# Weight sums moved one product ahead, z loaded into eight buffers, products of zeros before the first unit, and several steps of the first head moved

## The chip, the cores and the metric

The kernel runs on one core of a Trainium2 chip. The metric is the device time of one execution in microseconds; for the kernel before it is the median of three runs. A profile is one further execution with the hardware profiler on, and its span runs from the first to the last instruction that it recorded.

## The reference

One encoder layer on 528 rows of 2048 columns (16 meta tokens and 512 positions), cut here to what matters:

```
proj = h @ w_in                                  # u, g_ssm, q, k, v, g_sb, 1024 columns each
z    = gelu(s5_scan(u))                          # 64 groups of a diagonal state space model
hg   = z @ w_glu + b_glu
y_ssm = (hg[:, :1024] * sigmoid(hg[:, 1024:]) * silu(g_ssm)) @ w_branch_ssm
y_sb  = (stick_breaking_attention(q, k, v) * silu(g_sb)) @ w_branch_sb
gates = sigmoid(h @ w_gate + b_gate)             # 2048 x 4096 weights
mixed = gates[:, :2048] * y_ssm + gates[:, 2048:] * y_sb
out   = layer_norm(ALPHA * h + mixed @ w_out)
```

## The kernel before

Every operand of a large product is split into a high part (a cast to a narrower float32 form, on ScalarE) and a low part (the difference, on VectorE), and `mm3` issues three matmuls for each pair of operands: high by high, low by high, high by low. So each chunk of weights (128 by 1024, 512 KB, one DMA on SyncE's queue) needs a `copy` on ScalarE (line 171, tile `whi`) and a `split_lo` on VectorE (line 96, tile `wlo`) before TensorE can use it.

The work is a sequence of slots written by `slot()`. A slot uses one chunk in 8 pieces of 3 or more matmuls. At its start, `prep_upto` emits the copy and the split of the chunk that is used two slots later; the finish of the previous slot (`pend`) is emitted after that, or ahead of it where `soon=True`. At the fifth piece `load_upto` emits the DMA of the chunk five slots ahead. `schedule()` puts other work (VectorE tables, loads, the state space model, attention) at a piece number counted from the call. Each engine takes its instructions in the order in which they were emitted, and waits on data alone, so emission order is the whole schedule.

The stages in order: the first head's unit pair (u and v together, 16 pieces), its gate, k and q; then seven more heads, each with the state space and attention stages of the head before woven in; then eight units of g_ssm, in which the input is reloaded and its block sums are made for the next stage (`load_b`, `sums_b`); then the gates; then z times w_glu; the two branch products; and the output product with the layer norm.

The gates are 16 pairs (`pair(j)`), each seven products of 1024 by 128 weights on 256 columns (a seven-product scheme for a two by two block product). The order of the products is x = 0 to 6; x = 1, 2 and 3 use the block sums T2, T1 and T3, the others the input itself. The weight factors are: chunk 11 for x = 0; s2 = 21 + 22 - 11 for x = 1; s1 = 21 + 22 for x = 2; 11 - 21 for x = 3; 12 for x = 4; 12 - s2 for x = 5; 22 for x = 6. `factor()` (lines 142 to 161) emits the VectorE sums just ahead of the copy that needs them. The finishes e0 to e6 move results out of three accumulators: e0 is a ScalarE copy, e1, e3, e5 and e6 have VectorE additions, e3 to e6 a sigmoid on ScalarE, and e5 and e6 start a store from ScalarE's queue. Products x = 3, 5 and 6 accumulate onto an accumulator that an earlier finish has to read first.

During the last pair's x = 4, `open_z` frees the block sums and `load_z` (line 1177) is scheduled eight times, three pieces apart: a DMA of one 128 by 512 tile of z into a single buffer (`zt`, bufs=1), a copy on ScalarE (line 1180, `zh`) and a split on VectorE (`zl`). The stage that follows multiplies piece k by tile k of z.

In the first head, `params_v` (sines, cosines and an exponential, up to 52 scheduled steps on VectorE), `params_g` (on GpSimd) and `params_w` (a table of powers and its followers, up to 37 scheduled steps on VectorE) are put at pieces 10 to 26, 26 and 27 to 54 of the first head's 64 pieces. The splits of the input's 16 tiles (`split_x`, tiles `Xh`, `Xl`) are at pieces 0 to 13, tile c being needed at piece c. The first head's state space products s3 (line 750) and s5 (line 779) stand at pieces 44 and 50 of the second head; s5 needs the PSUM buffer that s3b empties with an addition (tile `X<-aux,dd`), and six 128 by 576 operations of `f3` on VectorE stand at piece 46, ahead of s3b.

Of the kernel before, what the change touches and what calls it, by code (L numbers as in the profile page):

```python
# [16 lines left out]
P = 128  # L17
# [11 lines left out]
NT = 8  # L29
# [9 lines left out]
def kernel(  # L39
# [55 lines left out]
    def tt(out, a, b, op, eng=V):  # L95
        eng.tensor_tensor(out, a, b, op)  # L96
# [29 lines left out]
    def load_upto(f):  # L126
        while issued[0] <= min(f, NFAC - 1):
            i = issued[0]
            pr = pair_of(i)
            if pr is None:  # L130
                raws[i] = load_raw(chunk_of(i))
            else:
                c = GATES + 4 * pr[0]
                w = sev.setdefault(pr[0], {})
                if pr[1] == 0:
                    w["11"], w["21"] = load_raw(c), load_raw(c + 2)
                    w["22"] = load_raw(c + 3, sev["p"], "r22", bufs=2)
                elif pr[1] == 1:
                    w["12"] = load_raw(c + 1)
            issued[0] += 1  # L140

    def factor(w, x):
        if x == 0:
            return w["11"]
        if x == 1:
            w["s1"] = sev["p"].tile([P, 1024], F32, tag="s1", name="s1")
            w["s2"] = sev["p"].tile([P, 1024], F32, tag="s2", name="s2")
            tt(w["s1"], w["21"], w["22"], ALU.add)
            tt(w["s2"], w["s1"], w["11"], ALU.subtract)
            return w["s2"]  # L150
        if x == 2:
            return w["s1"]
        if x == 3:
            tt(w["21"], w["11"], w["21"], ALU.subtract)
            return w["21"]
        if x == 4:
            return w["12"]
        if x == 5:
            tt(w["s2"], w["12"], w["s2"], ALU.subtract)
            return w["s2"]  # L160
        return w["22"]

    def prep_upto(f):
        while prepped[0] <= min(f, NFAC - 1):
            i = prepped[0]
            pr = pair_of(i)
            t = raws.pop(i) if pr is None else factor(sev[pr[0]], pr[1])
            hp, lp = held.get(i, (hi_p, lo_p))
            h = hp.tile([P, 1024], F32R, tag="hi", name="whi")
            lo = lp.tile([P, 1024], F32R, tag="lo", name="wlo")  # L170
            A.copy(h, t)  # L171
            split_lo(lo, t, h)
            his[i], los[i] = h, lo
            prepped[0] += 1
# [55 lines left out]
    with tc.manual_schedule():  # L230
# [48 lines left out]

        load_x(0, 1)  # L280
# [340 lines left out]
        def store_pv():  # L621
# [8 lines left out]
            + steps(gv_, 10, 26, 52)  # L630
            + [(26, lambda: drain(params_g()))]
            + steps(gw_, 27, 54, 37)
            + [(55, store_pv)]
# [64 lines left out]
        def ssm_stages(i):  # L698
# [147 lines left out]
            if i == 0:  # L846
                a = [(24, s1), (27, s1b), (29, s2(0)), (31, s2(1)), (33, s2(2)), (44, s3), (46, s3b), (52, s4)]
            return [(0, s0)] + a + [
                (50, s5), (52, s5a), (55, s5b), (57, s5c), (66, s7), (69, s7b), (71, s8), (74, s9)]
# [202 lines left out]
        for i in range(NT):  # L1052
# [52 lines left out]
            if i < NT - 1:  # L1105
                f1, f2, f3 = ssm_load(i + 1)
                schedule([(54, f1), (61, f3), (72, f2)])
# [69 lines left out]
        def load_z(j):  # L1177
            t = zst["p"].tile([P, S], F32, tag="zt", bufs=1, name="zt")
            SP.dma_start(out=t, in_=zd[j])
            A.copy(zst["h"][:, j, :], t)  # L1180
            split_lo(zst["l"][:, j, :], t, zst["h"][:, j, :])

        def pair(j):
# [46 lines left out]
            for x, (o, bh, bl, first_) in enumerate(ops):  # L1230
# [6 lines left out]
                if j == KT - 1 and x == 4:  # L1237
                    schedule([(0, open_z)] + [(1 + 3 * k, lambda k=k: load_z(k)) for k in range(NT)])
# [30 lines left out]
        def fin_ga(a, j):  # L1269
            hold["a"] = a  # L1270
            hold["t2"] = tmpl("zt")
# [261 lines left out]
```

## Time and profile before

| what | value |
|---|---|
| device time, median of 3 runs (lowest, highest) | 1505.92 us (1505.59, 1507.81) |
| the profiled execution's own time | 1507.89 us |
| its span, first to last instruction | 1506.1 us |
| granted TensorE clock, mean over the span | 0.988 |
| TensorE matmul busy | 1440.1 us (96%) |
| VectorE busy | 942.0 us (63%) |
| ScalarE busy | 482.0 us (32%) |
| GpSimd busy | 48.8 us (3%) |
| DMA | 196.50 MB, mean 130 GB/s |

Busy time counts a matmul from its start to the modelled end of its pipeline, so neighbouring matmuls overlap and a busy TensorE may still be spacing its matmuls too widely. The distance between the starts of neighbouring matmuls says more: it shows the clock and each wait. The clock is given as a share of 2.4 GHz, so 1.00 is the higher of its two levels and 0.50 the lower, 1.2 GHz.

### The profile page before, as it was taken

To read this page: it belongs to the slowest core of one execution; us is meant where nothing else is said; L and a number is where in the kernel's file an instruction comes from. 1 tells how busy PE (TensorE), PEld (TensorE's weight loads), DVE (VectorE), ACT (ScalarE), POOL (GpSimd) and SP (SyncE) were. 2 spreads that over 40 slices of the span, in tenths; PEclk is the share of its full clock that TensorE was granted. 3 is DMA by queue.
4 is the path that set the end of the run, shared out by engine and by line. 5 is a ranking of instruction groups with operands and counts; after the bars stand their busy time and mean duration, and the time that the engine had idled before them with its cause. 6 is when DMAs were issued, how large, how long until landed. Compare 5 with 4: busy or idle time off the path is not lost.

```text
span 1506.1 us, 22031 instructions
## 1 busy us (share of the span) xinstructions
PE 1440.1 (96%) x9040; PEld 1295.2 (86%) x9040; DVE 942.0 (63%) x1397; ACT 482.0 (32%) x764; POOL 48.8 (3%) x95
## 2 busy tenths in 40 slices
PE   7999999999999999998999999996999999999996
PEld 7989999999999898887999999995788888888885
DVE  8887767666767677577666666664454444423357
ACT  5322323233232323234444444433332222221120
POOL 0830000000000000000000000000000000000000
PEclk9999999999999999999999999998899999999998
DMA  7345253434434343462333233233454444474323
GB/s 250 117 129 142 85 141 96 135 105 118 126 114 107 113 116 118 122 219 92 121 131 125 100 133 133 95 124 120 160 150 151 141 151 134 136 208 153 98 98 112
DMA packets 96357, 196.50 MB, mean 130 GB/s; under 512 B 28416, under 2 KB 41984, under 8 KB 95488
## 3 DMA queue, kind: packets, MB, share of 16 engines
q1 hardware_dynamic: 77552, 177.20, 38.5%
q10 hardware_dynamic: 18704, 17.90, 3.5%
q8 instruction: 71, 1.16, 0.3%
q14 instruction: 30, 0.25, 0.1%
HBM read 172.78 MB, written 22.28 MB: 130 GB/s over the span
## 4 chain that ended last, share of the span: by engine, by line
PE 67%; DVE 17%; ACT 8%; issue 5%; DMA 2%; ACTq 0%; SPq 0%; DVEq 0%
PE acc L177 18%; PE acc L178 18%; PE acc L179 18%; ACT whi L171 6%; DVE wlo L96 5%; DVE s L96 4%; PE aux L177 3%; PE aux L179 2%; PE aux L178 2%; DVE u L96 2%; DVE raw L96 1%; DMA zt<-zd 1%; PE aux L818 1%; PE aux L779 1%; PE aux L814 1%
## 5 line engine op out<-in xcount | busy, mean ns | idle before, releaser
L177 PE MATMUL acc<-Xh,whi 128*128 128x256 f32 (+2 forms) x1664 | 520.9, 313 | 6.7 <-ACT whi L277 4.6
L96 DVE TENSOR_TENSOR wlo<-raw,whi 128x1024 fp32r<-128x1024 f32 (+1 forms) x242 | 294.9, 1220 | 362.6 <-ACT whi L171 355.4
L178 PE MATMUL acc<-Xl,whi 128*128 128x256 f32 (+2 forms) x1664 | 515.0, 309 | 2.3 <-DVE Xl L96 2.2
L179 PE MATMUL acc<-Xh,wlo 128*128 128x256 f32 (+2 forms) x1664 | 514.0, 309 | 0.0
L171 ACT CAST whi<-raw 128x1024 fp32r<-128x1024 f32 x238 | 247.7, 1049 | 463.6 <-PE acc L178 311.0
L177 PEld LDWEIGHTS acc<-Xh,whi 128*128 128x128 f32 x1664 | 316.3, 190 | 22.3 <-ACT whi L277 4.6
L178 PEld LDWEIGHTS acc<-Xl,whi 128*128 128x128 f32 x1664 | 316.0, 190 | 17.2 <-DVE Xl L96 3.5
L179 PEld LDWEIGHTS acc<-Xh,wlo 128*128 128x128 f32 x1664 | 315.6, 190 | 15.5
L96 DVE TENSOR_TENSOR wlo<-s,whi 128x1024 fp32r<-128x1024 f32 x48 | 58.8, 1225 | 69.8 <-ACT whi L171 69.8
L171 ACT CAST whi<-s 128x1024 fp32r<-128x1024 f32 x48 | 50.3, 1048 | 89.0 <-DVE s L96 81.5
L177 PE MATMUL acc<-zh,whi 128*128 128x512 f32 x128 | 53.2, 416 | 13.4 <-ACT zh L1180 7.8
L177 PE MATMUL acc<-T3h,whi 128*128 128x256 f32 x128 | 37.4, 292 | 17.4 <-DVE u L96 17.4
L178 PE MATMUL acc<-zl,whi 128*128 128x512 f32 x128 | 52.9, 413 | 0.3 <-DVE zl L96 0.2
L179 PE MATMUL acc<-zh,wlo 128*128 128x512 f32 x128 | 52.2, 408 | 0.0
L179 PE MATMUL acc<-oh,wlo 128*128 128x512 f32 x128 | 49.8, 389 | 0.0
L178 PE MATMUL aux<-wlo,mh 128*128 128x512 f32 x128 | 49.8, 389 | 0.0
L177 PE MATMUL aux<-whi,mh 128*128 128x512 f32 x128 | 49.8, 389 | 0.0
L179 PE MATMUL aux<-whi,ml 128*128 128x512 f32 x128 | 49.8, 389 | 0.0
L178 PE MATMUL acc<-wlo,mh 128*128 128x512 f32 x128 | 49.8, 389 | 0.0
L178 PE MATMUL acc<-sl,whi 128*128 128x512 f32 x128 | 49.8, 389 | 0.0
L178 PE MATMUL acc<-ol,whi 128*128 128x512 f32 x128 | 49.8, 389 | 0.0
L179 PE MATMUL acc<-sh,wlo 128*128 128x512 f32 x128 | 49.8, 389 | 0.0
(274 smaller groups left out, 2310.1 us busy)
## 6 DMA issues: line engine op xcount, KB each, us to landing
raw<-wst SPq DMA_DIRECT2D x238, 512.0 KB
gt<-gtd SPq DMA_DIRECT2D x32, 256.0 KB
xb<-xT SPq DMA_DIRECT2D x16, 264.0 KB
X<-brep SPq DMA_DIRECT2D x8, 512.0 KB
X<-pvd SPq DMA_DIRECT2D x16, 256.0 KB
X<-sd SPq DMA_DIRECT2D x8, 512.0 KB
gtd<-ga ACTq DMA_DIRECT2D x16, 256.0 KB
gtd<-gb ACTq DMA_DIRECT2D x16, 256.0 KB
```

The lines of the kernel that those rows point to most:

```text
L96: eng.tensor_tensor(out, a, b, op)
L171: A.copy(h, t)
L177: PE.matmul(o, ah, bh, start=start, stop=False, **kw)
L178: PE.matmul(o, ah, bl, start=False, stop=False, **kw)
L179: PE.matmul(o, al, bh, start=False, stop=stop, **kw)
L779: PE.matmul(vp[:, g, 0:NK], W["vt"][:, g].rearrange("p r q -> p (r q)"), ut[:, g * NK:g * NK + NK], start=True, stop=True,)
L814: PE.matmul(yp[:, g, 0:SK], W["ot"][:, g].rearrange("p t c -> p (t c)"), hs[:, g * NK + MK - 1:g * NK + MK - 1 + SK], start=True, stop=False,)
L818: PE.matmul(yp[:, g, 0:SK], W["mt"][:, g, :], ut[:, g * NK + MK:g * NK + MK + SK], start=False, stop=True,)
```

## The change

It does these things:

- The sums of the seven-product factors are emitted one product earlier than the copy that needs them: behind the ScalarE copy of the product before and ahead of its split. The loads follow: chunks 11 and 22 of a pair are now issued two slots earlier and chunk 21 one slot earlier, chunk 12 in the same slot as before; 22 goes ahead of 21.
- `zt` has eight buffers. All eight loads of z are issued at the start of the last pair's x = 4; the copies and splits come at pieces 10, 12 and so on to 22, and 23. The later user of the tag `zt` in `fin_ga` uses the eight buffers too.
- Ahead of the first loads a tile of zeros is set on VectorE and TensorE multiplies it 14 times, 256 columns each, into a PSUM tile that nothing reads.
- `params_v` goes to pieces 14 to 29, `params_g` to 29, `params_w` to 30 to 55, the store of its result from 55 to 56.
- For the first head s3, s3b and s4 move from pieces 44, 46, 52 to 47, 49, 55, and every state space step from s5 on moves by 3 pieces. For every head the loads and tables of the next head (f1, f3, f2) move from pieces 54, 61, 72 to 57, 62, 74.

```diff
@@ load_upto
-                if pr[1] == 0:
-                    w["11"], w["21"] = load_raw(c), load_raw(c + 2)
-                    w["22"] = load_raw(c + 3, sev["p"], "r22", bufs=2)
-                elif pr[1] == 1:
+                n_, x = pr
+                c = GATES + 4 * n_
+                w = sev.setdefault(n_, {})
+                nx = sev.setdefault(n_ + 1, {})
+                if i == GATES:
+                    load_first(w, c)
+                    load_second(w, c)
+                if x == 1:
                     w["12"] = load_raw(c + 1)
+                elif x == 5 and n_ < NSEV - 1:
+                    load_first(nx, c + 4)
+                elif x == 6 and n_ < NSEV - 1:
+                    load_second(nx, c + 4)
...
-    def factor(w, x):
...
+    def load_first(w, c):
+        w["11"] = load_raw(c)
+        w["22"] = load_raw(c + 3, sev["p"], "r22", bufs=2)
+
+    def load_second(w, c):
+        w["21"] = load_raw(c + 2)
+
+    summed = [GATES]
+
+    def sums_upto(f):
+        while summed[0] <= min(f, GATES + 7 * NSEV - 1):
+            n_, x = pair_of(summed[0])
+            w = sev[n_]
+            if x == 0:
+                w["s1"] = sev["p"].tile([P, 1024], F32, tag="s1", name="s1")
+                tt(w["s1"], w["21"], w["22"], ALU.add)
+            elif x == 1:
+                w["s2"] = sev["p"].tile([P, 1024], F32, tag="s2", name="s2")
+                tt(w["s2"], w["s1"], w["11"], ALU.subtract)
+            elif x == 2:
+                tt(w["21"], w["11"], w["21"], ALU.subtract)
+            elif x == 4:
+                tt(w["s2"], w["12"], w["s2"], ALU.subtract)
+            summed[0] += 1
+
+    FACTOR = ("11", "s2", "s1", "21", "12", "s2", "22")
@@ prep_upto
-            t = raws.pop(i) if pr is None else factor(sev[pr[0]], pr[1])
+            t = raws.pop(i) if pr is None else sev[pr[0]][FACTOR[pr[1]]]
...
             A.copy(h, t)
+            if GATES - 1 <= i + 1:
+                sums_upto(i + 1)
             split_lo(lo, t, h)
@@ ahead of load_x(0, 1)
+        wz = tp.tile([P, 256], F32R, name="wz")
+        V.memset(wz.bitcast(F32), 0.0)
+        wo_ = aux()
+        for _ in range(14):
+            PE.matmul(wo_[:, 0:256], wz[:, 0:P], wz, start=True, stop=True)
@@ first head's schedule
-            + steps(gv_, 10, 26, 52)
-            + [(26, lambda: drain(params_g()))]
-            + steps(gw_, 27, 54, 37)
-            + [(55, store_pv)]
+            + steps(gv_, 14, 29, 52)
+            + [(29, lambda: drain(params_g()))]
+            + steps(gw_, 30, 55, 37)
+            + [(56, store_pv)]
@@ ssm_stages
-                a = [..., (44, s3), (46, s3b), (52, s4)]
+                a = [..., (47, s3), (49, s3b), (55, s4)]
+            y = 3 if i == 0 else 0
             return [(0, s0)] + a + [
-                (50, s5), (52, s5a), (55, s5b), ...]
+                (50 + y, s5), (52 + y, s5a), (55 + y, s5b), ...]
@@ next head's loads
-                schedule([(54, f1), (61, f3), (72, f2)])
+                schedule([(57, f1), (62, f3), (74, f2)])
@@ load_z
-            t = zst["p"].tile([P, S], F32, tag="zt", bufs=1, name="zt")
+            t = zst["p"].tile([P, S], F32, tag="zt", bufs=NT, name="zt")
             SP.dma_start(out=t, in_=zd[j])
+            zst["t", j] = t
+
+        def split_z(j):
+            t = zst.pop(("t", j))
             A.copy(zst["h"][:, j, :], t)
             split_lo(zst["l"][:, j, :], t, zst["h"][:, j, :])
@@ pair(KT - 1), x == 4
-                    schedule([(0, open_z)] + [(1 + 3 * k, lambda k=k: load_z(k)) for k in range(NT)])
+                    schedule([(0, open_z)] + [(0, lambda k=k: load_z(k)) for k in range(NT)]
+                             + [(10 + 2 * k, lambda k=k: split_z(k)) for k in range(NT - 1)] + [(23, lambda: split_z(NT - 1))])
```

## Rows read from the trace of the kernel before

**Rows 1.** Busy time by stretch: start and end of the stretch, its length, then busy time and count for TensorE's matmuls, its weight loads, VectorE, ScalarE and GpSimd, the granted clock, the DMA share and GB/s. The stretches are part of the second head, a later head, the end of g_ssm, the 16 pairs of the gates, the start of z times w_glu, and a stretch of the branch products.

```profile
104.00:175.00 71.00, 68.06 (x486) 62.90 (x486) 57.22 (x90) 20.59 (x43) 0.00 (x0) 1.00 0.41 117
247.00:318.00 71.00, 71.00 (x506) 66.12 (x505) 49.24 (x79) 21.66 (x44) 0.00 (x0) 1.00 0.41 116
640.00:680.00 40.00, 36.98 (x175) 30.81 (x173) 29.69 (x61) 15.73 (x30) 0.00 (x0) 1.00 0.63 207
680.00:1030.00 350.00, 324.78 (x2622) 318.03 (x2623) 236.87 (x262) 147.36 (x196) 0.00 (x0) 1.00 0.34 118
1030.00:1065.00 35.00, 21.27 (x76) 14.52 (x76) 12.06 (x15) 10.28 (x16) 0.00 (x0) 0.67 0.36 114
...
1120.00:1260.00 140.00, 140.00 (x620) 115.95 (x619) 63.43 (x76) 37.39 (x43) 0.00 (x0) 1.00 0.45 148
```

**Rows 2.** Timeline of TensorE's matmuls around one pair of the gates: start, duration, line, tiles, and in brackets the idle time ahead and what ended it. The first and the last row are the first matmul of x = 1 in two neighbouring pairs; between them are the second matmul of x = 1, the third of x = 2 and the first of x = 3.

```profile
795.09 0.28 PE L177 MATMUL acc<-T2h,whi 128*128 128x256 f32 x1
795.21 0.28 PE L178 MATMUL acc<-T2l,whi 128*128 128x256 f32 x1
...
798.75 0.39 PE L179 MATMUL acc<-T1h,wlo 128*128 128x256 f32 x1 [0.38 <-DVE wlo L96]
...
802.66 0.35 PE L177 MATMUL acc<-T3h,whi 128*128 128x256 f32 x1 [1.01 <-DVE u L96]
...
817.12 0.28 PE L177 MATMUL acc<-T2h,whi 128*128 128x256 f32 x1
```

**Rows 3.** Timeline of VectorE in the same pair: the sums s1 and s2, the split of x = 2, the sum 11 - 21 with the split of x = 3, and the addition of e1.

```profile
790.25 1.22 DVE L96 TENSOR_TENSOR s<-raw 128x1024 f32<-128x1024 f32 x1
791.50 1.23 DVE L96 TENSOR_TENSOR s<-s,raw 128x1024 f32<-128x1024 f32 x1
...
797.47 1.22 DVE L96 TENSOR_TENSOR wlo<-s,whi 128x1024 fp32r<-128x1024 f32 x1 [2.02 <-ACT whi L171]
798.62 1.22 DVE L96 TENSOR_TENSOR raw<-raw 128x1024 f32<-128x1024 f32 x1
800.95 1.23 DVE L96 TENSOR_TENSOR wlo<-raw,whi 128x1024 fp32r<-128x1024 f32 x1 [1.11 <-ACT whi L171]
802.09 0.42 DVE L96 TENSOR_TENSOR u<-acc,p 128x256 f32<-128x256 f32 x1
```

**Rows 4.** Timeline of ScalarE in the same pair: the copy of x = 1 and the sigmoid of e6.

```profile
792.81 1.05 ACT L171 CAST whi<-s 128x1024 fp32r<-128x1024 f32 x1 [1.94 <-DVE s L96]
...
795.48 0.51 ACT L1198 ACTIVATE gb<-p,bga 128x256 f32<-128x256 f32 x1 [1.62 <-DVE p L96]
```

**Rows 5.** Timeline of all engines at the start of z times w_glu: a copy and a split of a tile of z, the stage's first matmul, and the first matmul of the stage after it.

```profile
1034.55 0.62 ACT L1180 CAST zh<-zt 128x512 fp32r<-128x512 f32 x1 [3.95 <-DMA zt<-zd]
1035.20 0.69 DVE L96 TENSOR_TENSOR zl<-zt,zh 128x512 fp32r<-128x512 f32 x1 [3.26 <-ACT zh L1180]
...
1040.58 0.80 PE L177 MATMUL acc<-zh,whi 128*128 128x512 f32 x1 [5.57 <-ACT whi L171]
...
1145.01 0.39 PE L177 MATMUL acc<-sh,whi 128*128 128x512 f32 x1
```

**Rows 6.** The chain of work that ended last, at the same place: start, length, what. Two of its DMA pieces.

```profile
1031.96 2.56 DMA zt<-zd
...
1035.92 2.66 DMA zt<-zd
```

**Rows 7.** Timeline at the change from g_ssm to the gates: a VectorE operation of a block sum, and TensorE's first matmuls of x = 1 and of x = 3 in the first pair.

```profile
664.92 0.43 DVE L96 TENSOR_TENSOR xb<-xb 128x256 f32<-128x256 f32 x1 [3.04 <-DMA xb<-xT]
...
678.82 0.39 PE L177 MATMUL acc<-T2h,whi 128*128 128x256 f32 x1 [2.35 <-ACT whi L171]
...
691.27 0.35 PE L177 MATMUL acc<-T3h,whi 128*128 128x256 f32 x1 [2.26 <-DVE u L96]
```

**Rows 8.** Timeline of TensorE in the first microseconds: the first matmul, two neighbours, and two that waited.

```profile
4.59 0.58 PE L177 MATMUL acc<-Xh,whi 128*128 128x256 f32 x1 [4.59 <-ACT whi L277]
...
6.61 0.41 PE L178 MATMUL acc<-Xl,whi 128*128 128x256 f32 x1
6.82 0.41 PE L179 MATMUL acc<-Xh,wlo 128*128 128x256 f32 x1
...
8.39 0.39 PE L178 MATMUL acc<-Xl,whi 128*128 128x256 f32 x1 [0.31 <-DVE Xl L96]
...
10.81 0.39 PE L177 MATMUL acc<-Xh,whi 128*128 128x256 f32 x1 [0.81 <-ACT Xh L255]
```

**Rows 9.** Timeline of TensorE in the first two heads: the longest wait for a split of the input, s3 and s5 (the count behind x is the number of matmuls merged into the row).

```profile
31.45 0.39 PE L178 MATMUL acc<-Xl,whi 128*128 128x256 f32 x1 [1.21 <-DVE Xl L96]
...
105.28 1.08 PE L750 MATMUL aux<-ot,bb 128*32 128x64 f32 x16 [1.25 <-DVE ot L96]
...
114.09 2.00 PE L779 MATMUL aux<-ut,vt 128*128 128x66 f32 x16 [1.70 <-DVE X L96]
```

**Rows 10.** Timeline of VectorE in the first two heads: the splits of two chunks of weights (for the first head's second half of q and the second head's first chunk), the first operation of `f3`, and the addition of s3b.

```profile
60.69 1.34 DVE L96 TENSOR_TENSOR wlo<-raw,whi 128x1024 fp32r<-128x1024 f32 x1 [0.45 <-ACT whi L171]
...
66.19 1.21 DVE L96 TENSOR_TENSOR wlo<-raw,whi 128x1024 fp32r<-128x1024 f32 x1
...
107.48 1.20 DVE L96 TENSOR_TENSOR tA<-ear,ebr 128x576 f32<-128x576 f32 x1
...
113.76 0.27 DVE L96 TENSOR_TENSOR X<-aux,dd 32x128 f32<-32x128 f32 x1
```

More of the change, by code (lines that the diff above doesn't have):

```diff
@@ L132, in load_upto @@
             else:
-                c = GATES + 4 * pr[0]
-                w = sev.setdefault(pr[0], {})
-                if pr[1] == 0:
-                    w["11"], w["21"] = load_raw(c), load_raw(c + 2)
-                    w["22"] = load_raw(c + 3, sev["p"], "r22", bufs=2)
-                elif pr[1] == 1:
+                n_, x = pr
[5 more added lines that the diff above has]
+                    load_second(w, c)
@@ L139, in load_upto @@
+                if x == 1:
                     w["12"] = load_raw(c + 1)
+                elif x == 5 and n_ < NSEV - 1:
+                    load_first(nx, c + 4)
+                elif x == 6 and n_ < NSEV - 1:
+                    load_second(nx, c + 4)
             issued[0] += 1
-    def factor(w, x):
[L143 to L161, printed above, removed]
+    def load_first(w, c):
+        w["11"] = load_raw(c)
+        w["22"] = load_raw(c + 3, sev["p"], "r22", bufs=2)
@@ L846, in ssm_stages @@
             if i == 0:
-                a = [(24, s1), (27, s1b), (29, s2(0)), (31, s2(1)), (33, s2(2)), (44, s3), (46, s3b), (52, s4)]
+                a = [(24, s1), (27, s1b), (29, s2(0)), (31, s2(1)), (33, s2(2)), (47, s3), (49, s3b), (55, s4)]
+            y = 3 if i == 0 else 0
             return [(0, s0)] + a + [
-                (50, s5), (52, s5a), (55, s5b), (57, s5c), (66, s7), (69, s7b), (71, s8), (74, s9)]
+                (50 + y, s5), (52 + y, s5a), (55 + y, s5b), (57 + y, s5c), (66 + y, s7), (69 + y, s7b), (71 + y, s8), (74 + y, s9)]
         SCALE = 1.0 / float(P) ** 0.5
@@ L1270, in fin_ga @@
             hold["a"] = a
-            hold["t2"] = tmpl("zt")
+            hold["t2"] = tmpl("zt", NT)
             SP.dma_start(out=hold["t2"], in_=gd[j])
```

## The prediction

> **What bounds the kernel now.** I read the busy times by stretch first [rows 1]. In a late head TensorE is busy in all 71.00 us of 71.00 and in the branch products in 140.00 of 140.00, both at a clock of 1.00; there nothing on another engine can shorten the time. Three stretches differ. The 16 pairs of the gates have 324.78 us busy of 350.00, the start of z times w_glu 21.27 of 35.00 with a clock of 0.67, and the second head 68.06 of 71.00. The change edits these three, and the first microseconds.
>
> The timeline of one pair shows what is lost in the gates [rows 2]. Neighbouring matmuls start 0.12 us apart (795.09, 795.21). A pair has 7 x 8 x 3 = 168 of them, so 20.16 us if none waits; the pairs' period is 817.12 - 795.09 = 22.03. The 1.87 us between lie at two places: 0.38 us ahead of the third matmul of x = 2, which wants its split, and 1.01 ahead of x = 3, which wants the addition of e1 (the rest of the 1.87 is the pipeline refilling). Why they are late is on VectorE [rows 3] and ScalarE [rows 4]: s1 and s2 (790.25, 791.50) precede the copy, which waits 1.94 us for them, and the split waits for the copy. A step later the sum for x = 3 (798.62) ends, its copy starts, its split stands at 800.95, and e1's 0.42 us comes behind that, at 802.09. Sum, copy and split follow one another, and neither engine is full.
>
> In the z stage the copies and splits alternate with loads [rows 5, 6]: a copy waits 3.95 us for its load, each load takes 2.56 to 2.66 us and starts only when the single buffer is free. The first matmul waits 5.57 us, so the stage's idle starts at 1040.58 - 5.57 = 1035.0, and the next stage starts at 1145.01: 110.0 us for 16 x 8 x 3 = 384 matmuls. At the spacing of the branch products, 140.00 / 620 = 0.226 us [rows 1], they take 86.7. So 23.3 us are lost, part of it as the low clock.
>
> **The change, part by part.** First the sums. Put t = 0 at the start of x = 4; a slot is 24 x 0.12 = 2.88 us, and what is prepared in one slot is used two slots later. With the durations of rows 3 and 4 (sum 1.23, split 1.22, addition 0.42, copy 1.05, sigmoid 0.51) I fill both queues in the new order. Slot x = 4: e3's two additions, the copy of x = 6, the next pair's s1, the split, done at 3.8. Slot 5: s2 and the split of the next x = 0, done at 6.2. Slot 6 (from 5.8): e5, the sum 11 - 21, the split of x = 1, done at 9.4, wanted at 11.5. Slot 0: e6 and the split of x = 2, done at 12.7, wanted at 14.4. Slot 1: 12 - s2 and the split of x = 3, done at 15.2; e1 follows at 15.6; wanted at 17.3. Slots 2 and 3 have one split each, done at 16.9 and 19.6, and at 20.2 VectorE is free for the next e3. Every margin is over 1.5 us, so both waits go and the pair takes 20.16 us. VectorE's work stays the same, some 15 us of the 20. Fifteen pairs by 1.87 give **28.0 us**. Bounds: 0.76 of each (x = 2 alone cured) and all of it.
>
> The loads move with them. Behind SyncE's queue head the riskiest is 21: its buffer is free when x = 3 is split, at 15.2, and s1 wants it at 21.0. A load of half its size took 2.66 us [rows 6]; between 2.66 and twice that, 5.3, it lands by 20.5 either way. 11, 22 and 12 have a slot more. Cost 0, covered by these 0.5 us or more and by the 1.7 us of margin behind.
>
> The first pair is apart. VectorE is behind with the block sums: x = 1 waits 2.35 us and x = 3, at 691.27, 2.26 us [rows 7]. Now s1 fills 1.2 of the 3.04 us that VectorE waited for a load at 664.92, and the sums no longer stand ahead of copies. Following both queues from there I get x = 3 at some 688 to 690 in place of 691.27. What holds it is the remaining block sums. Nearest to the middle I take **3 us**; bounds 0.5 and 7.
>
> The z stage: all eight loads are issued when x = 4 of the last pair starts (t = 0). The first lands after 2.6 us; the others, an estimate from 256 KB at the 207 GB/s of the stretch 640 to 680 [rows 1], 1.27 apart, the last at 11.5 (bounds: all at 2.6, or 2.6 apart). Copies (0.62) and splits (0.69) come behind the last copies of the gates: tiles 0 to 2 done by 7.5, then e5 and the next chunk's copy hold ScalarE until 9.9, tile 3 is split at 11.7, tile 7 at 14.1. The stage starts at 8.6 and wants tile 3 at 10.9, then one every 0.68: some 0.9 us late at tile 3, none after. TensorE no longer stands still, so the clock stays up. Gain 23.3 - 0.9 = **22.4 us**; bounds 14.6 (below) and 23.3. Eight buffers for t2 remove a possible wait and add no instruction: 0.
>
> The zeros: 14 matmuls at the low clock's spacing of 0.21 us [rows 8] are 2.9 us, before the first real matmul at 4.59, which waits for a load anyway: no cost. What they give: with the clock up, the first piece's 12 matmuls finish 12 x 0.09 = 1.1 us sooner. But the next ones wait for the splits and casts of later input, at 8.39 and 10.81 [rows 8], whatever the clock. I take **0**; bounds a gain of 1.1 and, if the longer wait lets the clock fall again, a loss of the same 1.1.
>
> The Trainium skill, "TensorE: Matmul & The Clock Gate", Part 1, says that the array starts throttled and that sustained activity releases it. By that rule the zeros take the slow start on themselves, and the sum would be 1.1 us lower; the trace agrees on the slow start (0.21 us at 6.61) and not on the gain (the wait at 8.39).
>
> The first head: the splits of input tiles 12 to 15 come ahead of the phases, so the waits for tiles 13 to 15, of which the 1.21 us at 31.45 is the longest [rows 9], go: between 1.2 and 3.6 us, I take 2. VectorE's work is the same, though, and its queue sets this part: three power steps (six operations of 64 columns, each at most the 0.42 us of 256 columns [rows 3], some 2 us) now follow the split at 60.69, which waits for ScalarE's copy, in place of preceding it. So the split at 66.19 comes some 2 us later [rows 10], and TensorE, 2 us early, waits for it. Net 0. s3 three pieces later loses its wait of 1.25. s5 loses part of its 1.70 [rows 9]: it needs the addition at 113.76 behind six operations of about 1.2 us from 107.48 [rows 10], and now a split of 1.2 us comes between. Together I take **0.6 us**; bounds a loss of 2 and a gain of 5. GpSimd's drain and the store only move in order; their users come a head later. f1, f3 and f2 of later heads move by 3, 1 and 2 pieces under a TensorE that has no idle time there [rows 1], with two slots of cover; without it 0.7 us for each of seven heads.
>
> **Sum**: 28.0 + 3 + 22.4 + 0 + 0.6 = 54.0 us. The profiled execution took 1507.89 (span 1506.1 and 1.8 around it), so 1453.9; the median of the three runs is 1.97 lower, so **1452 us**. About 0.2%, or 3 us, is what a measurement can tell from no change.
>
> **Rivals.** (a) The z loads land one after another even with eight buffers, as they do now at 2.6 each: tile 7 lands at 20.8 and is split at 22.1, where 13.6 was wanted, so 8.7 us are lost and the time is 1460. For it: the chain shows only DMA pieces there. Against it: each waited for its buffer. Chance 0.13. (b) A wait stays in every pair, because e1 or a split still queues behind another operation: half of the 1.87 us is 14, so 1466. For it: e1 ran right behind a split; against it: the margins. Chance 0.12. (c) The warm start pays 12 x 0.09 us: 1451. For it the spacing of 0.21 [rows 8], against it the wait for data at 8.39. Chance 0.07. The Trainium skill's page named above would have it so. (d) Slower than before: s1 now waits on VectorE for chunk 21, and behind it stand the split of x = 6 and all later ones. It decides from a load of 21 that takes over 7.5 us; every further microsecond costs 15 us, and at 12 us the time is 1452 + 15 x 4.5 = 1520. The 2.66 us for half the size [rows 6] speaks against it. Chance 0.03, of which 0.01 ends near no change. (e) The moves of the first head do not do what they are put there for, and only push VectorE's backlog on: a loss of 2, 1455. Chance 0.06. The forecast keeps 0.59.
>
> **Numbers.** The forecast's own bounds are 1445 (the first pair at 7, the head at a gain of 3.5) and 1458; (a), (c) and (e) are added to that, most of (b) is left out: 1445 to 1462. Faster by over 0.2%: all but (d), 0.97; within 0.2%: 0.01; slower: 0.02.
>
> **What would show it.** Right: starts of x = 1 in neighbouring pairs 20.2 us apart with no idle ahead of x = 2 and x = 3; the copies of the factors no longer waiting for sums; at the z stage a clock of 1.00, and under 2 us between the last gate matmul and full spacing; 8.39 and 10.81 unchanged. Wrong: a period over 20.5, copies of z that wait for loads, a clock of 0.5 in the z stage, or s5 with its full wait.

## The result, and the profile after

The changed kernel takes 1456.34 us in the median of four runs (1454.76 to 1457.04), the kernel before 1506.51 on the same chip: ratio 0.9665, 95% interval 0.9648 to 0.9682, so about 50 us less. The prediction was 1452.0 with a range of 1445 to 1462. The profiled execution takes 1456.62 us (span 1454.8), 51.3 less than the one that the prediction summed against.

Busy times by stretch, in the columns of [rows 1]: the second head, a later head, the end of g_ssm, the pairs of the gates, the start of z times w_glu, and the branch products.

```profile
104.00:175.00 71.00, 69.45 (x478) 64.12 (x476) 57.48 (x89) 20.48 (x43) 0.00 (x0) 0.98 0.42 117
247.00:318.00 71.00, 71.00 (x503) 66.10 (x501) 49.06 (x80) 21.67 (x44) 0.00 (x0) 1.00 0.43 117
640.00:680.00 40.00, 37.82 (x178) 31.36 (x176) 28.44 (x60) 15.65 (x30) 0.00 (x0) 1.00 0.62 212
680.00:1005.00 325.00, 320.97 (x2655) 320.19 (x2656) 239.12 (x268) 151.78 (x200) 0.00 (x0) 0.99 0.40 134
1005.00:1040.00 35.00, 34.25 (x156) 28.24 (x156) 18.30 (x24) 14.96 (x22) 0.00 (x0) 1.00 0.57 191
1090.00:1230.00 140.00, 140.00 (x619) 115.99 (x618) 64.90 (x77) 34.98 (x39) 0.00 (x0) 1.00 0.46 147
```

The gates now have 4 us without a matmul where they had 25, all of them in the first pair, and the z stage starts at full clock (1.00, was 0.67).

One pair, TensorE, the answer to [rows 2]: first matmul of x = 1, third of x = 2, first of x = 3, first of x = 1 of the next pair.

```profile
790.40 0.28 PE L194 MATMUL acc<-T1h,wlo 128*128 128x256 f32 x1
...
793.04 0.28 PE L192 MATMUL acc<-T3h,whi 128*128 128x256 f32 x1
...
807.44 0.28 PE L192 MATMUL acc<-T2h,whi 128*128 128x256 f32 x1
```

No bracket, so no wait: x = 2's third matmul follows its second (790.28) by 0.12 us. All fourteen distances between neighbouring pairs from the second pair on are 20.16 us. VectorE over the same time, the answer to [rows 3]; it works ahead, for the next pair: s1, s2, the sum 11 - 21, the split of x = 2, and e1 after the split of x = 3.

```profile
796.91 1.22 DVE L96 TENSOR_TENSOR s<-raw 128x1024 f32<-128x1024 f32 x1
...
799.65 1.22 DVE L96 TENSOR_TENSOR s<-s,raw 128x1024 f32<-128x1024 f32 x1
...
802.25 1.22 DVE L96 TENSOR_TENSOR raw<-raw 128x1024 f32<-128x1024 f32 x1
...
807.94 1.23 DVE L96 TENSOR_TENSOR wlo<-s,whi 128x1024 fp32r<-128x1024 f32 x1 [2.02 <-ACT whi L184]
...
811.35 0.42 DVE L96 TENSOR_TENSOR u<-acc,p 128x256 f32<-128x256 f32 x1
```

Each sum stands one product ahead of the copy that reads it, and s1 waits for no load. The z stage, the answer to [rows 5]: ScalarE's copies, which no longer wait for loads; then TensorE's first matmul, its only wait (tile 3), and the first matmul of the next stage.

```profile
1001.91 1.66 ACT L1206 CAST zh<-zt 128x512 fp32r<-128x512 f32 x3
...
1007.35 2.70 ACT L1206 CAST zh<-zt 128x512 fp32r<-128x512 f32 x5
```

```profile
1006.16 0.40 PE L192 MATMUL acc<-zh,whi 128*128 128x512 f32 x1
...
1009.36 0.50 PE L193 MATMUL acc<-zl,whi 128*128 128x512 f32 x1 [0.75 <-DVE zl L96]
...
1094.28 0.39 PE L192 MATMUL acc<-sh,whi 128*128 128x512 f32 x1
```

The stage takes 88.12 us instead of 110.0. That leaves the two places where the sum was less sure. The first pair, the answer to [rows 7]: VectorE, then SyncE's queue, then TensorE at x = 1 and x = 3.

```profile
664.57 1.23 DVE L96 TENSOR_TENSOR s<-raw 128x1024 f32<-128x1024 f32 x1 [2.95 <-DMA raw<-wst]
...
671.24 0.42 DVE L96 TENSOR_TENSOR xb<-xb 128x256 f32<-128x256 f32 x1 [1.59 <-DMA xb<-xT]
```

```profile
666.96 0.33 SPq L123 DMA_DIRECT2D raw<-wst  x1
667.34 7.83 SPq L1158 DMA_DIRECT2D xb<-xT  x6
```

```profile
682.25 0.58 PE L194 MATMUL acc<-T2h,wlo 128*128 128x256 f32 x1 [1.84 <-DVE wlo L96]
...
692.18 0.36 PE L192 MATMUL acc<-T3h,whi 128*128 128x256 f32 x1 [1.01 <-ACT whi L184]
```

s1 waits 2.95 us for chunk 21, and with it the split of chunk 95, the last ahead of the gates, behind it on VectorE. Chunk 12's load wants the buffer of chunk 95, so SyncE stands there until 666.96; the loads of the block sums are queued behind it, and VectorE then waits for them too. The start and the first heads, the answers to [rows 8, 9]: waits for the second and the third input tile, for the first gate, for two splits of weights, for the first attention products, and s5.

```profile
8.93 0.39 PE L193 MATMUL acc<-Xl,whi 128*128 128x256 f32 x1 [0.34 <-DVE Xl L96]
...
11.34 0.39 PE L192 MATMUL acc<-Xh,whi 128*128 128x256 f32 x1 [0.79 <-ACT Xh L270]
...
33.85 0.50 PE L192 MATMUL acc<-Xh,whi 128*128 128x512 f32 x1 [0.57 <-ACT us L1078]
...
63.24 0.50 PE L194 MATMUL acc<-Xh,wlo 128*128 128x512 f32 x1 [0.53 <-DVE wlo L96]
...
69.80 0.39 PE L194 MATMUL acc<-Xh,wlo 128*128 128x256 f32 x1 [1.06 <-DVE wlo L96]
...
108.25 0.38 PE L193 MATMUL aux<-atl,vh 16*128 16x256 f32 x1 [1.02 <-DVE atl L96]
...
117.77 1.45 PE L800 MATMUL aux<-ut,vt 128*128 128x66 f32 x12
```

The gate starts at 33.85 where it started at 35.46, s5 has no wait; but the waits at 63.24 and 69.80 are new, and so is the one at 108.25.

### The profile page after: what moved, and what is told of

Read it like the earlier page. It is cut to its first block, busy times and chain, and to the rows that moved or that the text cites. A ratio compares the mean times of both kernels' runs of the same rounds, so it can differ in the third digit from the quotient of the medians.

```text
span 1454.8 us, 22053 instructions
## 1 busy us (share of the span) xinstructions
PE 1427.9 (98%) x9054; PEld 1293.4 (89%) x9054; DVE 938.1 (64%) x1398; ACT 482.8 (33%) x764; POOL 47.6 (3%) x95
## 4 chain that ended last, share of the span: by engine, by line
PE 90%; DVE 6%; DMA 2%; issue 1%; ACT 1%; SPq 0%; DVEq 0%; ACTq 0%
PE acc L192 25%; PE acc L193 25%; PE acc L194 25%; PE aux L192 3%; PE aux L193 3%; PE aux L194 3%; DVE wlo L96 1%; PE aux L839 1%; PE aux L800 1%; PE aux L835 1%; PE aux L947 1%; DMA xt<-xT 1%; PE aux L771 1%; ACT whi L184 1%; DMA raw<-wst 1%
## 5 line engine op out<-in xcount | busy, mean ns | idle before, releaser
L193 PE MATMUL acc<-zl,whi 128*128 128x512 f32 x128 | 49.9, 390 | 0.7 <-DVE zl L96 0.7
L192 PE MATMUL acc<-zh,whi 128*128 128x512 f32 x128 | 49.8, 389 | 0.0
L192 PE MATMUL acc<-sh,whi 128*128 128x512 f32 x128 | 49.8, 389 | 0.0
L192 PE MATMUL acc<-oh,whi 128*128 128x512 f32 x128 | 49.8, 389 | 0.0
L192 PE MATMUL acc<-whi,mh 128*128 128x512 f32 x128 | 49.8, 389 | 0.0
L194 PE MATMUL acc<-whi,ml 128*128 128x512 f32 x128 | 49.8, 389 | 0.0
```

Of the source, the lines that this page charges most:

```text
L192: PE.matmul(o, ah, bh, start=start, stop=False, **kw)
L193: PE.matmul(o, ah, bl, start=False, stop=False, **kw)
L194: PE.matmul(o, al, bh, start=False, stop=stop, **kw)
```

## The experiments

The median of the kernel before differs by up to 0.14% between chips, so each time has its ratio to the kernel before on the same chip. The marks below place a difference: **M** is the first matmul of s5 in the last head, **P** the first matmul of x = 1 in the second pair, **S** the first after the z stage. (The expectation of best_a calls s5's first matmul an "s3-type mark".)

| kernel | median us | ratio, 95% | M | P | S |
|---|---|---|---|---|---|
| before | - | 1 | 612.47 | 706.66 | 1145.01 |
| changed | 1456.34 | 0.9665, 0.9648-0.9682 | 613.39 | 706.64 | 1094.28 |
| z_only | 1487.03 | 0.9857, 0.9838-0.9876 | 614.08 | 708.57 | 1124.89 |
| sums_only | 1477.59 | 0.9803, 0.9789-0.9816 | 611.69 | 707.19 | 1114.76 |
| old_loads | 1456.06 | 0.9653, 0.9639-0.9666 | 611.84 | 705.68 | 1093.35 |
| no_zeros | 1457.87 | 0.9666, 0.9650-0.9682 | 613.23 | 706.87 | 1094.5 |
| old_head | 1458.36 | 0.9669, 0.9654-0.9684 | 612.76 | 708.30 | 1095.9 |
| first_pair | 1455.58 | 0.9650, 0.9634-0.9666 | 612.09 | 705.99 | 1093.6 |
| pool_sums | 1453.87 | 0.9641, 0.9627-0.9654 | 611.69 | 703.12 | 1090.74 |
| head_order | 1454.55 | 0.9641, 0.9628-0.9655 | 611.47 | 704.60 | 1092.23 |
| first_halves | 1454.43 | 0.9646, 0.9633-0.9659 | 612.99 | 703.93 | 1091.61 |
| best_a | 1452.55 | 0.9633, 0.9620-0.9646 | 610.41 | 701.54 | 1089.23 |
| best_b | 1450.54 | 0.9620, 0.9607-0.9633 | 609.35 | 699.44 | 1087.15 |
| best_c | 1449.20 | 0.9615, 0.9602-0.9628 | 609.03 | 699.02 | 1086.70 |

**The z stage alone (z_only).** The kernel before with `bufs=NT`, the eight loads together and `split_z`:

```diff
-    schedule([(0, open_z)] + [(1 + 3 * k, lambda k=k: load_z(k)) for k in range(NT)])
+    schedule([(0, open_z)] + [(0, lambda k=k: load_z(k)) for k in range(NT)] + [... split_z ...])
```

> The kernel before with the z stage's part of the change alone (eight buffers, loads issued together, splits in later slots). Theory (the parts add up): the stage from the first zh to the first sh takes 88.1 us as in the changed kernel, 21.9 less than before, and nothing else moves: 1506.5 - 21.9 = 1484.6 us, ratio 0.9855. Rival (the loads go one after another): 2.6 us apart, about 8 us worse, 1492.5. Rival (the z stage only gained because the gates ended with TensorE dense): a clock of 0.5 again at its start, 10 us or more of the gain lost, over 1494.

From P to S it takes 416.32 us where the kernel before takes 438.35: 22.0 less, and 0.9857 is 21.6 us. The stage itself takes 88.8 us, 0.7 more than the theory had. The theory holds; the loads did not go one after another.

**The sums alone (sums_only).** The kernel before with `sums_upto`, `load_first`, `load_second` and the factor table, and nothing else.

> The kernel before with the sums a product ahead and their loads moved, and nothing else. Theory (the parts add up): the 15 pairs 20.16 us apart with no wait, 28.7 us less between the second pair's start and the z stage; the first pair within 1.5 us of the changed kernel's 26.73; the z stage still with loads one after another and a clock near 0.67, 110 us or up to 2 more, since the gates end sooner and not its loads; together 1506.5 less 28 to 30, 1477.5 us, ratio 0.981. Rival (the z stage's loss grows by what the gates gain at their end): 1482 or more. Rival (the pairs keep a wait without the other edits): a period over 20.5 and over 1482.

The ratio is as the theory had it, and 0.9857 x 0.9803 = 0.9663 against 0.9665 for the whole change. No matmul of pairs 2 to 16 waits. The z stage, alone with its old loads, starts with the low clock and half-empty as before (the stretch in the columns of [rows 1]; below it the first matmul):

```profile
1005.00:1040.00 35.00, 22.73 (x71) 15.00 (x70) 10.23 (x13) 9.69 (x14) 0.00 (x0) 0.71 0.41 139
```

```profile
1011.25 0.79 PE L192 MATMUL acc<-zh,whi 128*128 128x512 f32 x1 [4.38 <-ACT whi L184]
```

From P to S it saves 30.8 us; z_only's 22.0 and these make 52.8, the whole change 50.7. So the parts overlap by 2.1 us, and the overlap lies in the z stage: with its old loads it takes 107.9 us here, counted from the end of the last gate matmul, where it took 110.0, and not the 110 to 112 of the theory. The medians can't resolve so little.

**The loads back in their old slots (old_loads).**

```diff
-    if i == GATES: load_first(w, c); load_second(w, c)
-    if x == 1: w["12"] = ...
-    elif x == 5 ...: load_first(nx, c + 4)
-    elif x == 6 ...: load_second(nx, c + 4)
+    if x == 0: w["11"], w["21"], w["22"] = ...
+    elif x == 1: w["12"] = ...
```

> The changed kernel with the sums a product ahead, but the loads back in their old slots: 11, 21 and 22 at x = 0 and 12 at x = 1. Theory (the order on VectorE is what pays; the loads have slack): s1 is due 21.0 us after the start of x = 4, three loads issued together at 16.2 land by about 22.7 if they share one after another, 1.7 us of margin stand behind: period 20.2 to 21.0, 1456 to 1468 us. Rival (the loads' move is half of the gain): VectorE waits for the load of 21 in every pair by over 3 us, period 21.5 or more, over 1476. Rival (the old slots are better for the first pair, whose queue then has the block sums' loads ahead): 1453 to 1455.

From P to S 387.67 us against 387.64: the period stays at 20.16. In two of the fifteen later pairs s1 waits for a load, by 0.60 and 0.65 us, and no matmul waits for it. The order on VectorE pays; moving the loads was worth nothing here. The prediction had put the move at no cost; it brought no gain either.

**Without the zeros (no_zeros).** The memset and the loop of 14 matmuls taken out.

> The changed kernel without the fourteen products of zeros. Theory (worth nothing, since the second group of matmuls waits for data): 1456.3 us within 0.5, with the gate unit of the first head starting at the same 33.9 us; the first group at 0.21 us spacing, the waits that followed it at 8.2 and 11.3 us in the changed kernel longer or equal. Rival (warm start pays, as rival c of the prediction): 1.1 us slower, 1457.4, and every later mark 1.1 us later. Rival (the zeros delay the start): the first split of x tile 1 at 7.0 us in place of 7.5, the later marks 0.5 us earlier, 1455.8.

0.9666 against 0.9665: no difference, but intervals of 2.4 us to either side can't tell 1.1 us from nothing. The marks of the start can. The zeros do bring the full spacing forward; neighbouring matmuls of the first piece, in the changed kernel (with the wait that follows) and without the zeros:

```profile
6.48 0.28 PE L193 MATMUL acc<-Xl,whi 128*128 128x256 f32 x1
6.60 0.28 PE L194 MATMUL acc<-Xh,wlo 128*128 128x256 f32 x1
...
8.20 0.38 PE L192 MATMUL acc<-Xh,whi 128*128 128x256 f32 x1 [0.94 <-ACT Xh L270]
```

```profile
6.69 0.41 PE L193 MATMUL acc<-Xl,whi 128*128 128x256 f32 x1
6.91 0.41 PE L194 MATMUL acc<-Xh,wlo 128*128 128x256 f32 x1
```

They start 0.12 us apart with the zeros and 0.22 without, and what is won so is spent in the wait for the cast of the second input tile. The first gate starts at 33.68 us without the zeros, at 33.85 in the changed kernel, and between 33.34 and 33.94 in all nine kernels that have both the zeros and the new first head. The start varies by itself: in the changed kernel the second input tile is cast at 7.53 us where it was at 6.99, and the waits at 8.39 and 10.81 of [rows 8] move to 8.93 and 11.34; but best_c below, with the same zeros, has them where the kernel before had them:

```profile
8.39 0.39 PE L195 MATMUL acc<-Xl,whi 128*128 128x256 f32 x1 [0.34 <-DVE Xl L96]
10.81 0.38 PE L194 MATMUL acc<-Xh,whi 128*128 128x256 f32 x1 [0.81 <-ACT Xh L272]
```

So the warm start does not pay here, and a delay by the zeros does not show.

**The first head's moves back (old_head).** Powers, drain, store, f1 to f3 and s3 to s9 in their old pieces, the rest as changed.

> The changed kernel with the phases, powers, drain, store and the first head's later products back in their old places; sums, z and zeros as changed. Theory (the moves are worth 0.9 us, which the changed trace shows at the start of head 2): 1457.3 us, s5 of the first head with a wait near 1.7 us and s3 near 1.2, waits for x tiles 13 to 15 back. Rival (the 0.9 us comes from the zeros, and the moves only pass the wait on): no later mark moves by more than 0.3 us, 1456.3. Rival (the moves cost, since the wait went to the first attention products and dropped the clock there): 1455.3 or less, and clock 1.00 between 108 and 112 us.

0.9669 against 0.9665 decides nothing, and M is earlier, not later. What decides M is the clock. After the waits near 108 us (or at s5, in the old order) TensorE's granted clock falls to 1.2 GHz in some executions and not in others, by the same instructions of the first head. Stretches of four kernels, in the columns of [rows 1]: changed, then old_loads (same first head), then z_only and the kernel before (same first head).

```profile
108.00:112.00 4.00, 3.75 (x19) 3.37 (x20) 3.93 (x6) 0.00 (x0) 0.00 (x0) 0.59 0.42 131
```

```profile
108.00:112.00 4.00, 3.90 (x36) 3.52 (x37) 3.93 (x6) 0.00 (x0) 0.00 (x0) 1.00 0.47 131
```

```profile
116.00:120.00 4.00, 4.00 (x23) 4.00 (x23) 3.40 (x5) 2.23 (x6) 0.00 (x0) 0.57 0.11 23
```

```profile
116.00:120.00 4.00, 4.00 (x36) 4.00 (x36) 3.50 (x5) 2.61 (x8) 0.00 (x0) 1.00 0.11 19
```

With the new moves and a clock of 1.00 there, M is 612.09, 611.84, 611.69 (first_pair, old_loads, pool_sums); with 0.59, 0.62, 0.69 it is 613.39, 613.23, 612.99 (changed, no_zeros, first_halves). With the old moves and 1.00 it is 612.47, 612.76, 611.69 (before, old_head, sums_only), with 0.57 it is 614.08 (z_only). At equal clock the means differ by 612.31 - 611.87 = 0.4 us in favour of the moves, but the three old values lie 1.1 us apart and the three new ones 0.4, so this is not told from nothing. The fall is: from the wait at 108 us to M it takes 505.1 to 505.2 us in the three that fell and 503.7 to 503.8 in the others, 1.4 more; from the first head's s5 to M it takes 499.9 in z_only and 498.3 to 498.4 in the others with the old moves, 1.5 more.

**The first pair's loads (first_pair).**

```diff
-    load_first(w, c); load_second(w, c)     # i == GATES
+    load_second(w, c); load_first(w, c)
-    if x == 1: w["12"] = ...
+    if x == (3 if n_ == 0 else 1): w["12"] = ...
```

> The changed kernel with two loads of the first pair in another order: chunk 21 ahead of 11 and 22, and chunk 12 two products later, behind the block sums' loads. Theory (in the first pair s1 waits for chunk 21, and the load of chunk 12, which waits for a buffer, holds the block sums' loads on the queue): s1's wait of 2.95 us falls under 1, the block sums' loads issue near 662.3 again, the waits of 1.8 us at x = 0 and x = 1 shrink, and x = 3 starts 2 to 4 us earlier: 1452.5 to 1454.5 us. Rival (VectorE's block sums alone hold the first pair, whatever the loads): x = 3 within 0.5 us of 692.18, 1456. Rival (another load becomes the late one): slower by up to 1 us.

Only half of the theory holds. s1 still waits 2.92 us, and the edit could not cure that: s1 adds 21 and 22, and 22 is now the last of the three. But the block loads now go out at once:

```profile
658.92 14.25 SPq L1158 DMA_DIRECT2D xb<-xT  x8
```

and x = 1's split comes 2.0 us earlier (TensorE 680.25, was 682.25; s1 starts at 664.53 and 664.57, so the times compare). x = 3 comes 1.04 us earlier, not 2 to 4, and P only 0.65. The next wait, for x = 2's copy, grows from 0.42 to 1.54 us, and the clock stays low for longer (679 to 691 us; changed, then this kernel):

```profile
679.00:691.00 12.00, 8.64 (x53) 7.78 (x51) 10.42 (x17) 7.66 (x13) 0.00 (x0) 0.86 0.32 109
```

```profile
679.00:691.00 12.00, 8.43 (x46) 7.78 (x47) 10.42 (x17) 7.00 (x12) 0.00 (x0) 0.76 0.37 128
```

**Block sums partly on GpSimd (pool_sums).** first_pair's edits, s1 a product later, and:

```diff
-    tt(t4 row, b21, b22, ALU.subtract)
+    tt(t4 row, b21, b22, ALU.subtract, G)
-    for x, b_ in (("1", b11), ("3", b12), ("2", b22)): split_lo(...)
+    tt(T3l row, b12, T3h row, ALU.subtract, G)
+    for x, b_ in (("1", b11), ("2", b22)): split_lo(...)
```

> The changed kernel with three edits at the transition to the gates: the load order of the run before it (21 ahead of 11 and 22, chunk 12 two products later), the first pair's s1 behind the split of chunk 95 in place of ahead of it, and two of the eight VectorE operations of each block sum (the t4 difference and the split of T3) given to GpSimd. Theory (in the first pair VectorE's work in a row is the bound: 11.69 us busy of 12 there): 16 x 0.34 = 5.4 us less on VectorE, less what GpSimd delays by slower operations (0.74 us for 128x256 in the phases); the waits at x = 0 to 2 fall below 0.5 us each, the clock does not fall to 1.2 GHz, and the second pair starts 5 to 9 us earlier than 706.64: 1447.5 to 1452 us. Rival (each wait is replaced by one for ScalarE or for a block load): 1454 to 1456. Rival (GpSimd holds the block buffers, so the loads come later): 1457 or more.

P comes 3.5 us earlier (1.8 from M), short of the theory's 5 to 9, and the clock still falls (0.57 from 684 to 688 us). Little of it comes by the work given away. VectorE's operations beside GpSimd's, then GpSimd's:

```profile
656.23 1.83 DVE L96 TENSOR_TENSOR xb<-xb 128x256 f32<-128x256 f32 x3
657.98 0.42 DVE L96 TENSOR_TENSOR T1l<-xb,T1h 128x256 fp32r<-128x256 f32 x1
658.53 0.74 DVE L96 TENSOR_TENSOR T2l<-xb,T2h 128x256 fp32r<-128x256 f32 x1
```

```profile
658.14 0.86 POOL L96 TENSOR_TENSOR t4r<-xb 128x256 f32<-128x256 f32 x1 [1.28 <-DVE xb L96]
```

A split of 0.42 us takes 0.74 and three operations of 1.33 take 1.83 while GpSimd works: from 656.23 to 659.27 this block sum holds VectorE for 3.04 us, and the changed kernel's, with all its operations on VectorE, from 658.82 to 661.62, for 2.80. (These are seven; the expectation's eight is a miscount.) Over all eight block sums VectorE is busy with them for 20.1 us in place of 21.5, but s1, the sum 11 - 21 and one split beside GpSimd take 1.71, 1.70 and 1.43 us in place of 1.23, 1.22 and 1.23, which takes back 1.2 of the 1.4. The Trainium skill, "Perfetto Trace Analysis", section "Optimizing Scalar/DVE Operations", says that VectorE and GpSimd share a read port and that moving work between the two might not help; the trace agrees (0.42 against 0.74 us). What is left to have helped, by exclusion, is the order: s1, which no longer holds the block sums up, and SyncE's queue, free as in first_pair; the run does not part the two.

**The first head's products once more (head_order).**

```diff
-    y = 6 if h == 0        # attention pieces from the first transpose on
+    y = 8 if h == 0
-    schedule([(3, f2), (4, f1), (46, f3), ...])
+    schedule([(3, f2), (4, f1), (50, f3), ...])
```

> The changed kernel with two moves more in the first head: the third load and its products (f3) four pieces later, the attention pieces from the first transpose on two pieces later. Theory (the wait that s3 lost went to the first attention products, 0.52 and 1.02 us, since the splits of at stand behind other VectorE work; the clock falls behind these waits and costs 1.2 us more): the waits at 106.87 and 108.25 fall below 0.3 us together, the clock stays at 1.00 between 108 and 112 us, and all later marks come 1.5 to 2.7 us earlier: 1453.6 to 1454.8 us. Rival (VectorE's work is the bound there, and any order of it leaves the same sum of waits): later marks within 0.5 us, and the wait shows at s5: 1456. Rival (f3 late makes s4 or s5 late): slower by 1 us or more.

The theory holds: both waits are gone (one of 0.26 us is left at 119 us), the clock stays up, and M is 1.92 us before the changed kernel's, of which 1.4 is the clock. In the profiled executions of all four kernels with these moves, this one and best_a to best_c, the clock is 1.00 there.

```profile
108.00:112.00 4.00, 4.00 (x39) 3.62 (x39) 2.24 (x4) 2.01 (x5) 0.00 (x0) 1.00 0.39 139
```

**The transition rearranged (first_halves).** Block sums two pieces earlier and four apart, their inputs as halves in five buffers, s1 a product later and the first pair's sums behind the split, the gate's store on GpSimd's queue.

```diff
+    split_lo(lo, t, h)
+    if GATES <= i < GATES + 7: sums_upto(i + 1)
...
-    A.dma_start(out=gd[j], in_=t)
+    G.dma_start(out=gd[j], in_=t)
...
-    (86 + 5 * c, ... sums_b(c))
+    (84 + 4 * c, ... sums_b(c))
```

> The changed kernel with the transition to the gates alone rearranged: block sums from two pieces earlier and four pieces apart in place of five, their inputs loaded as halves with five buffers in place of two whole ones; in the first pair the sums behind the split of their product in place of ahead of it, s1 a product later, chunk 12 two products later; the store of the gate's product issued from GpSimd, so that ScalarE's queue does not wait there for VectorE. Nothing is given to GpSimd to compute. Theory (the first pair's loss is VectorE's queue, block sums late because their loads are late, and the low clock that follows each wait of over a microsecond): x = 1 no longer waits 1.8 us for its split nor x = 2 and x = 3 for their copies; the clock stays at 1.00 from 679 to 691 us; from the last s5-type mark of the heads to the second pair's start 86 to 89 us in place of 93.25: 1449 to 1452.5 us. Rival (the memory of the heads, freed by two late stores, holds the first block sum at 649 us whatever is loaded earlier, and the rest follows): 91 to 93 us, 1454 to 1456. Rival (the earlier block loads delay the weights' loads): a new wait for a weight load ahead of 676 us, 1457 or more.

M to P takes 90.94 us in place of 93.25, and the median falls less than the theory had it. The rival is in part right: the first block sum still waits for a store of the last head and ends at 649.9 us, where it ended at 650.5. VectorE then waits 3.38 us, until 665.30, for a block load that was issued behind three weight loads. The theory's low clock behind each wait of over a microsecond does not hold throughout: the kernel before has 1.00 from 104 to 112 us, though s3 waits 1.25 us there [rows 9].

**All together (best_a, best_b, best_c).** best_a adds head_order to first_halves; best_b puts the last power steps back in pieces 27 to 54; best_c issues the first pair's loads of 11, 22 and 21 one product later.

```diff
-    + steps(gw_, 30, 55, 37)       # best_b
+    + steps(gw_, 27, 54, 37)
-    if i == GATES:                 # best_c
+    if i == GATES + 1:
```

> The run before this one with the first head's two moves of the run head_order as well. Theory (the parts add up): the s3-type mark of the second head near 185.3 us, no fall of the clock between 108 and 112 us, and 1 to 2 us less than the run before it: 1447.5 to 1451.5 us. Rival (the head's gain is the clock's chance and no part of the median): the same time as the run before it within 0.7.

> The run before this one with the last power steps back in their old pieces, 27 to 54. Theory (at 63.2 and 69.8 us the changed kernel waits for splits whose copies stand behind ScalarE's sigmoids and VectorE's powers; with the powers earlier VectorE is free later): the two waits of 0.53 and 1.06 us fall below 0.8 together, 0.5 to 1 us less than the run before it. Rival (the powers then hold the splits of the last input tiles, and waits ahead of 34 us come back): same or up to 1 us slower.

> The kernel of the run best_b with the first pair's loads of 11, 22 and 21 one product later. Theory (in best_b VectorE stands idle for 3.5 us at 657.5 us, since the block loads are issued behind those three weight loads and share the DMA engines with them; from there to x = 1 VectorE works without a break, so x = 1's wait of 2.73 us for its copy is that idle time passed on): the idle time at 657.5 us falls under 1, x = 1 waits under 0.5 us, and the second pair starts 2 to 3.4 us earlier than best_b's 90.09 us after the last s5 mark of the heads: 1447 to 1448.5 us. Rival (s1 and s2 stand between x = 1's copy and the rest, and chunk 21 now lands late for them): a wait for that load on VectorE, and 1450.5 or more.

best_a is 1.9 us under first_halves, at 1452.55 above its range of 1447.5 to 1451.5; s5 of the second head starts at 184.25 (186.83 there) and the clock is 1.00 at 108 to 112 us. best_b loses the wait near 69.8 us and keeps the one at 63 (0.57); the second head's s5 is 1.04 us earlier, as expected. M is 1.06 us earlier, so nothing is lost or won between the second head and the last. The median fell by 2.0: the intervals of the ratios overlap, but on their one chip best_b's runs (1449.63 to 1451.15) all lie below best_a's (1451.57 to 1452.93). Another 1.0 us of it arises between M and P, where the two kernels do not differ. best_c's theory fell: VectorE's idle time did not go, it moved to a later block load,

```profile
667.04 0.89 DVE L96 TENSOR_TENSOR xb<-xb 128x256 f32<-128x256 f32 x2 [3.00 <-DMA xb<-xT]
```

and x = 1 waits 2.73 us as before. best_c, above its 1447 to 1448.5, is no better than best_b by its marks (M to P 89.99 and 90.09), but both beat the changed kernel: 0.9615 (0.9602 to 0.9628) lies below 0.9665 (0.9648 to 0.9682).

## Why the prediction was right, and where its sizes were off

- **The sums**, 28.0 us: 328.3 us from P to the z stage became 299.5, 28.8 less. Both waits went, and by the mechanism that the prediction named: its splits, due at 3.8, 6.2, 9.4, 12.7 and 15.2 us after the start of x = 4, end at 3.8, 6.1, 9.7, 13.3 and 15.5 in the pair shown. The least margin is 1.2 us, not over 1.5. The lower bound of 0.76 us for x = 2 alone reads 0.65 by the starts of that pair before. old_loads shows that the order on VectorE did it.
- **The z stage**, 22.4 us: 21.9. One wait was left, at tile 3, of 0.75 us where 0.9 was worked out; tiles 3 and 7 are split 11.8 and 14.2 us after the start of x = 4, due at 11.7 and 14.1. The clock of 1.00 is part of it: with the old loads the stage starts at 0.71 (sums_only).
- **The zeros**, 0: shown by the start of no_zeros, not by its median. Rival (c) falls: the zeros do bring the full spacing forward, but the next matmuls wait for input whatever the clock. So the sum by the rule of the Trainium skill, "TensorE: Matmul & The Clock Gate", Part 1, was 1.1 us too low.
- **The first pair**, 3 us, was mis-sized: it measured 0.9 from M to P in the profiled pair of executions, and with the same first-pair edits sums_only and old_head have 95.50 and 95.54 us where the kernel before has 94.19, so it is not to be told from nothing. x = 3, forecast at 688 to 690, came at 692.18, 78.8 us behind M as before. The step that failed is "s1 fills 1.2 of the 3.04 us that VectorE waited": s1 itself waits for a load, and the prediction, which weighed 21's load only in the later pairs, did not follow SyncE's queue in this one, where chunk 12's load waits for a buffer ahead of the block loads. first_pair shows that this cost 2.0 us at x = 1. What then holds the pair stays open: the later runs rearrange the block loads and the order on VectorE and ScalarE together, and x = 1 still waits 2.73 us in best_c.
- **The first head**, 0.6 us: at equal clock 0.4, within the spread, in the profiled execution -0.9, since the clock fell at 108 us. The gate started 1.6 us earlier where 2 was taken. The prediction had the split near 66 us coming 2 us later (it came at 68.54) and s5 losing part of its wait, but not that the wait would go to the first attention products.
- Rivals (a), (b) and (d) are refuted by the z copies, the period, and s1 without a wait after the first pair. (e) is half right: the first head's wait was passed on.

The sum was 54.0 us and the profiles differ by 51.3. The two big terms were put at 50.4 and made 50.7 (P to S); the two small ones were put at 3.6 and made nothing (P at 706.66 and 706.64); the stages after S gained 0.5 that nobody had counted. The other 1.7 of the 4.4 us between 1451.9 and 1456.3 are the step from execution to median: 1.97 was taken off, as for the kernel before, and in the changed kernel it is 0.28.

## What to carry to other kernels

Where two engines feed a third in turn and neither is full, put each operation one step ahead of its reader, and check the order on the queue before the loads: here the order was worth 28.8 us and the loads' slots nothing. At a transition, follow every queue through: one load that waits for a buffer holds all behind it, and the gain of an edit ends there. A term under 2 us next to short waits can't be read from one execution; read it by marks, at equal clock, from more than one.

## What the runs showed that was not expected

- The clock may fall or not after the same short waits: 0.59 to 0.69 at 108 to 112 us in three executions of the new first head, 1.00 in three others; it costs 1.4 us. A cure that shortens one wait and leaves another may come with a longer time at low clock (first_pair, 0.76 where the changed kernel has 0.86, one execution each).
- A VectorE operation with two inputs took up to 1.8 times as long beside GpSimd (0.74 us in place of 0.42).
- In the first microseconds the granted clock reads 1.00 though the matmuls of that stretch start 0.21 us apart [rows 8], as they do at a granted clock of 0.50 (first_pair, 688 to 692 us); the spacing is the better witness. The stretch, of the kernel before:

```profile
6.20:8.00 1.80, 1.80 (x9) 1.61 (x8) 0.35 (x1) 0.79 (x3) 0.00 (x0) 1.00 1.01 369
```
